# A two-layer RWKV-7 and gMLP trunk: new places and banks in the loop, low-rank products by split halves, gate values projected with tokens on partitions

## The chip, the cores and the metric

The kernel runs on one core of a Trainium2 chip. The metric is the device time of one execution in microseconds, the median over several runs. The engines are TensorE (PE in the profile; its weight loads are PEld), VectorE (DVE), ScalarE (ACT), GpSimd (POOL) and SyncE (SP), which here issues the DMAs (queue SPq).

## The reference

The kernel computes one inference step of two layers with model width D = 1024 and mixer width E = 2048. A prompt of 512 tokens and 8 sample sequences of 4 tokens (32 rows) share the weights. Layer 0 is RWKV-7 time mixing with 32 heads of 64, layer 1 a chunked gMLP.

```python
# layer 0 (h = RMSNorm(x)); sh: first 6272 of 8320 columns, z: the last 2048
proj = h @ w_in
xm = sh + (prev - sh) * mu                   # prev: the token before
r, k, v, wd, ad = split(xm)                  # 2048, 2048, 2048, 64, 64
wf = w0 + tanh(wd) @ w2                      # low-rank products
a  = sigmoid(a0 + ad @ a2)
decay = exp(-exp(-softplus(-wf) - 0.5))
S_t = S_{t-1} diag(w_t) + (S_{t-1} (-kk_t)) (kk_t*a_t)^T + v_t k_t^T
y_t = S_t r_t                                # per head, then group norm, bonus
x  = x + ((norm(y) + bonus) * silu(z)) @ w_out

# layer 1 (h = RMSNorm(x)), chunks of 128 tokens, 8 groups of 256 features
u, v, z = gelu(h @ w_u), gelu(h @ w_v), h @ w_z
v = layernorm(v) * v_g + v_b                 # over the 2048 features of a token
mixed = tril(ws[g]) @ v[chunk, g] + bs       # along the tokens of a chunk
x = x + (u * mixed * silu(z)) @ w_out
```

The outputs are the two final RMSNorms (prompt and sample), the last shifted row and the final matrix state of every sequence, and the sample rows of v.

## The kernel before

**Layout.** The 544 tokens lie on the free axis in two halves of 272 columns (256 prompt, 16 sample); features lie on the 128 partitions. A projection takes a block of 128 features: the weights are the stationary operand and the tokens move. Every fp32 weight and activation is split into a high half (`w_h`, `hh`) and the remainder (`w_l`, `hl`), both of the type fp32r, and a product is made of three matmuls, high x high, high x low, low x high (`mm3`, L249 to L252). `halves` (L115) makes the two halves of a block of weights: a copy on ACT and a subtraction on DVE. A projection of 128 features is 2 halves x 8 blocks of depth x 3 = 48 such matmuls of 272 columns.

**The head** (up to some 40 us) loads x and all constants, norms the tokens, turns them (`pth`) and writes `hh` and `hl`.

**The loop** (some 40 to 730 us) runs over 16 pairs of heads p. Each pair has four projections (k, r, v, z: 192 matmuls), and a list of smaller stages written as generators, which yield after each operation. The names of their PSUM tiles are those of the profile: `plw` and `pla` are the low-rank products (`lora`, L418; 64 rows deep, in fp32, two at once in the upper and lower half of the array), `pge`/`pgo` the Gram products inside a chunk, `pm1` to `pm4` and `pak` the inversion by blocks, `pz`, `pm`, `pn` and `sb` (L795 on) what carries the state from chunk to chunk, `py` the outputs, `psm`, `psy`, `pst`, `psu` the sample rows and their state, `pss` the norms, `pxt` turns of x for later. `pz`, `pm`, `pn`, `py` and the others of a pair of heads use tiles of 64 rows or 64 columns of the array (in the profile 64*128, 128*64 and so on ahead of the shape); `pgs`, `pms` and `pvs` further on use 32.

**What sets the order.** A table `AT` gives for every stage the places of its steps, in units of which a pair of heads has 64 (one unit for 3 matmuls of the projections). All steps are sorted by place into one agenda, and the program is emitted in that order on PE, DVE, ACT, POOL and SP; each engine and queue then works in order. `BANKS` says which of the PSUM banks a stage's tile lies in. After the loop, the output projection (`po`, `out_stream`) is woven in with the last stages: the junction, 720 to 780 us.

**The second layer** first projects the gate values (gv, 16 blocks of 128 features). A block's evacuation (`vevac`, L1223) multiplies by the norm factor `bc` on DVE and applies Gelu on ACT, and one block later `vturn` turns it: four transposes of 128x128 (`pvt`, L1235) into `Vt` with tokens on partitions, and one of the 32 sample rows (`pvs`, L1238) into `Vs`. Then statistics, and blocks of gu and gz (272 columns each) with the mixing between: `mix` (L1301) multiplies `Vt` by the 128x128 mixing matrix `wst` (`pmx`) and the sample rows `Vs` by a 32x32 one, `wsx` (`pms`). Last comes the output projection (go, and `pgl` at the end with 256 moving columns; `pgs` for its sample rows, in four tiles of 128x32 of the array) and the final norm.

Of the kernel before, what the change touches and what calls it, by code (L numbers as in the profile page):

```python
# [14 lines left out]
D = 1024  # L15
# [14 lines left out]
BANKS = {'plw0': 'wa', 'plw1': 'g', 'pla0': 'sm', 'pla1': 's', 'pss': 'g', 'pge0': 'g', 'pge1': 'wa', 'pgo0': 's', 'pgo1': 'wa', 'pbo0': 's', 'pbo1': 'g', 'pbk0': 'g', 'pbk1': 's', 'pv': 'y', 'pat': 'wa', 'pak': 'sm', 'pxt': 'sm', 'psu': 'wa', 'pm1': 'y', 'pm2': 'wa', 'pm3': 'sm', 'pm4': 'sm', 'ps0': 'wa', 'pit': 'wa', 'psy': 'sm', 'pst': 's', 'pso': 'wa', 'psm': 'y'}  # L30
# [36 lines left out]
def build(tc, A, O, off):  # L67
# [5 lines left out]
    with ctx:  # L73
# [62 lines left out]
        with tc.tile_pool(name="st", bufs=1) as st:  # L136
# [13 lines left out]
            Q.dma_start(cst, A["consts"])  # L150
# [4 lines left out]
            raws_in[1] = load_in(1)  # L155
            r1 = st.tile([113, 128], F32, name="r1")
# [45 lines left out]
            mss = [stats(0), stats(1)]  # L202
            V.tensor_scalar(xsh, xs, mss[0][0:32, 2:3], None, op0=ALU.mult)
            scale(0)
            wts0 = halves(*raws_in.pop(0))
            for h in range(2):
                for k in range(KD):
# [10 lines left out]
                    if h == 0 and k == 4:  # L218
                        scale(1)

# [137 lines left out]
        def pcol(col, p):  # L358
            return col[:, p : p + 1]
# [49 lines left out]
        lx = lH.tile([128, 2, HT], F32, name="lx")  # L409
        xl = hd("xl", "h1")  # L410

        def lora_in():
            for js, src in ((slice(0, 256), xl[:, 0:512].rearrange("p (h j) -> p h j", h=2)), (slice(256, 272), xl[:, 512:544].rearrange("p (h j) -> p h j", h=2))):
                S.activation(lx[e_, :, js], src[e_], AF.Tanh)
                S.activation(lx[o_, :, js], src[o_], AF.Copy)
            yield

        def lora(p):  # L418

            z = Z[p]  # L420
            lr = lH.tile([128, 128], F32, name=f"lr{p}", tag="lr", bufs=2)
            for n, rs in (("rw_w2", e_), ("rw_a2", o_)):
                Q.dma_start(lr[rs], A[n][0, :, 128 * p : 128 * p + 128])
            yield
            for h in range(2):
                ps = [bk(f"pl{n}{h}", p)[:, 0:HT] for n in "wa"]
                for x, rs in zip(ps, rw_):
                    T.matmul(x, lr[rs], lx[rs, h, :], start=True, stop=True)
                yield
                if h == 0:  # L430
                    xa = z["xa"] = hd(f"xa{p}", "h1")
                for x, dp_, ds_, bcol in ((ps[0], pv(xw), sv(xw), pcol(w0h, p)), (ps[1], cpv(xa), csv(xa), pcol(w0h, 16 + p))):
                    S.activation(dp_[:, 4 * h : 4 * h + 4, :], x[:, 0:256].rearrange("p (c j) -> p c j", j=64), AF.Tanh, bias=bcol, scale=0.5)
                    S.activation(ds_[:, 4 * h : 4 * h + 4, :], x[:, 256:272].rearrange("p (c j) -> p c j", j=4), AF.Tanh, bias=bcol, scale=0.5)
                    yield
# [536 lines left out]
        def tail(p):  # L972
# [59 lines left out]
            wk=(-24.6703, -13.9502, -10.5009),  # L1032
            wr=(-1.92923, 4.85448, 5.61825),
            wv=(0.606097, 15.3323, 15.3323),
            wz=(26.5557, 37.8471, 43.6636),
            sk=(0.789221, 8.8031, 15.711, 15.8424, 17.6719, 17.7726, 18.4403),
            sr=(7.54549, 28.6206, 31.674, 31.674, 34.0009, 34.0009, 38.5955),
            sv=(43.7782, 45.1654, 47.4232, 49.7307, 49.7307, 51.0746, 55.203),
            sl=(-48.6951, -2.31874, 1.08412, 4.68622, 4.68622, 4.68622, 4.68622),
            lin=(5.21945,),  # L1040
            kpost=(24.9494, 25.986, 25.986, 25.986, 26.4478, 26.4478, 26.4478, 28.1479, 28.7234, 28.9758, 46.1589),
            norms=(26.5963, 27.2646, 42.3595, 42.3595, 43.7228, 43.7228),
            norms0=(30.3638, 36.1029, 36.1029, 42.7321, 43.0652, 43.81),
            rpost=(34.2118, 40.034, 43.0665, 59.6417),
            gram=(38.5207, 38.5207, 38.5207, 38.5207, 38.5507, 38.7256, 44.4019, 46.8335, 55.0017),
            vpost=(57.36,),
            bonus=(47.1621, 50.0087, 67.1245, 68.9711, 69.0871, 71.7472),
            gate=(58.7304, 58.7304, 68.9911, 70.1851, 70.432, 104.018),
            keys=(51.7578, 52.1495, 90.6263, 93.0718),
            sides=(71.9966, 73.0768, 73.0768, 79.7128, 89.332),  # L1050
            lora=(-37.6497, -16.243, -12.6778, -6.32377, -6.32377, -5.15096, 0.12609, 0.958916, 8.84795, 19.5291, 19.5291, 39.8259),
            lora0=(-48.6977, 9.64576, 9.64576, 9.68669, 9.68669, 9.68669, 9.68669, 9.68669, 9.69389, 18.8347, 22.6537, 30.7022),
            lanes=(4.59191, 56.0959, 56.1972, 56.1972, 57.7957, 57.8272, 57.8272, 59.1798, 61.4444, 61.4444, 61.7838, 61.7838, 63.4843, 63.4843, 64.0257, 64.7786, 65.5865, 65.5865, 68.1234, 68.1534, 76.599, 78.8691),
            merge=(89.9516, 90.29, 91.6755, 91.6755, 93.2448, 94.0464, 94.0464, 99.0064, 99.0064, 102.136, 102.373),
            smp=(4.36649, 64.2531, 73.5271, 79.3115, 79.3115, 82.6169, 82.6169, 82.6169, 84.1463, 84.509, 88.3156, 89.5629, 89.5629, 90.1406, 90.873, 93.3779, 94.0364, 99.466, 102.52, 102.958, 103.396, 105.645, 115.209, 116.915, 116.947, 124.943, 129.788, 136.306, 191.625),
            chain=(102.988, 102.988, 102.988, 102.988, 103.098, 104.998, 104.998, 105.819, 111.041, 111.599, 111.599, 111.599, 111.85, 111.85, 111.85, 114.008, 114.008, 114.008, 114.008, 115.066, 115.066, 115.284, 116.962, 118.608, 120.078, 121.408, 121.557, 123.546, 124.856, 128.208, 128.208, 129.056, 129.056, 129.056, 129.847, 129.965, 129.965, 147.17),
            tail=(132.502, 132.502, 132.572, 132.98, 132.98, 141.147, 141.337, 146.854, 147.433, 159.083, 159.098, 163.745, 164.046, 166.048, 166.166, 166.34, 168.968, 171.692),
            flip=(115.408, 135.41, 142.071, 165.144),
# [116 lines left out]
        with tc.tile_pool(name="l1", bufs=1) as l1, tc.tile_pool(name="l1t", bufs=2) as lt, tc.tile_pool(name="ob1", bufs=4) as ob:  # L1175
# [19 lines left out]
            bl = [(0, 0, 128), (0, 128, 128), (1, 0, 128), (1, 128, 128), (0, 256, 16), (1, 256, 16)]  # L1195
            for i, (h, a, n) in enumerate(bl):
                T.matmul(ps[0:n, i : i + 1], acc[:, h, a : a + n], ones[:, 0:1], start=True, stop=True)
            rs1 = l1.tile([128, 6], F32, name="rs1")
            V.tensor_scalar(rs1[:, 0:4], ps[:, 0:4], 1.0 / D, NORM_EPS, op0=ALU.mult, op1=ALU.add)
            V.tensor_scalar(rs1[0:16, 4:6], ps[0:16, 4:6], 1.0 / D, NORM_EPS, op0=ALU.mult, op1=ALU.add)  # L1200
            G.tensor_tensor(out=rs1[:, 0:4], in0=rs1[:, 0:4], in1=nhalf[:, 0:4], op=ALU.pow)
            G.tensor_tensor(out=rs1[0:16, 4:6], in0=rs1[0:16, 4:6], in1=nhalf[0:16, 0:2], op=ALU.pow)
            bc = l1.tile([128, 2, HT], F32, name="bc")
            for h in range(2):
                ps = wa("pbc")
                for i, (hh_, a, n) in enumerate(bl):
                    if hh_ == h:
                        dg = lt.tile([128, 128], F32, name=f"dg{i}", tag="dg")
                        V.tensor_scalar(dg[0:n, 0:n], ident[0:n, 0:n], rs1[0:n, i : i + 1], None, op0=ALU.mult)
                        T.matmul(ps[:, a : a + n], ones[0:n, :], dg[0:n, 0:n], start=True, stop=True)  # L1210
                S.activation(bc[:, h, :], ps[:, 0:HT], AF.Copy)
# [3 lines left out]
            Vs = l1.tile([32, E], F32, name="Vs")  # L1215
# [3 lines left out]
            for f in range(NF):  # L1219
                vT = lt.tile([128, 2, 256], F32, name=f"vT{f}", tag="gz", bufs=3)  # L1220
                vTs = lt.tile([128, 2, 16], F32, name=f"vTs{f}", tag="vTs")

                def vevac(h, ps, f=f, vT=vT, vTs=vTs):  # L1223
                    a = lt.tile([128, HT], F32, name=f"va{f}", tag="va")
                    V.tensor_tensor(out=a, in0=ps, in1=bc[:, h, :], op=ALU.mult)
                    S.activation(vT[:, h, :], a[:, 0:256], AF.Gelu_apprx_tanh)
                    S.activation(vTs[:, h, :], a[:, 256:272], AF.Gelu_apprx_tanh)

                project(f"gv{f}", G_IN, E + 128 * f, vevac)

                def vturn(f=f, vT=vT, vTs=vTs):
                    ps = wa("pvt")
# [13 lines left out]
                if f:  # L1246
                    late()
# [257 lines left out]
```

## Time and profile before

| | before |
|---|---|
| median of 3 runs | 1301.79 us (1300.9 to 1302.03) |
| the profiled execution: its own time, its span | 1303.13 us, 1301.3 us |
| mean granted TensorE clock | 0.996 |
| PE busy | 1272.5 us (98%), 14860 matmuls |
| DVE, ACT, POOL busy | 961.2 (74%), 690.9 (53%), 126.6 (10%) |
| DMA | 123.24 MB, 95 GB/s in the mean |
| PE waiting longest | png on a DMA at the start 8.2; po on DVE's o_l 2.4; pth on xsh 1.7 |

The times below are those of the profiled execution. A line of the timeline or of the groups has the source line, engine, operation, the tile written and the tiles read, for a matmul the part of the array (rows * columns) where it is given, and the shape. The busy time of a matmul includes its way through the array, so successive matmuls overlap, and the distance from start to start says what one costs.

### The profile page before, as it was taken

The numbers are of one execution on the slowest core, as the hardware profiler recorded it, in microseconds if no ns is written. First come the engines' busy times: TensorE is split into PE (matmuls) and PEld (weight loads), VectorE is DVE, ScalarE is ACT, GpSimd is POOL, SyncE is SP. The second block draws the span as 40 slices with busy tenths as digits, with TensorE's granted clock in tenths as the row PEclk, the third lists the DMA queues.
The fourth block names the chain that finished last, engine by engine and source line by source line (L and its number), as shares of the span: only waits on it lengthen the run. The fifth ranks groups of instructions, "written<-read, shape, count | busy, mean of one in ns | idle before, by whom it ended". The sixth has DMA issues, their size and how long they took to land.

```text
span 1301.3 us, 35878 instructions
## 1 busy us (share of the span) xinstructions
PE 1272.5 (98%) x14860; PEld 1200.1 (92%) x14860; DVE 961.2 (74%) x2231; ACT 690.9 (53%) x1612; POOL 126.6 (10%) x346
## 2 busy tenths in 40 slices
PE   6999999999999999999999989999999999999997
PEld 5899999999998999899999879999999999999997
DVE  5688888888888888888888866474448656656466
ACT  5766667667666766766677453254333223232333
POOL 1122011111211110111112100000000000000000
PEclk9999999999999999999999999999999999999999
DMA  4522342433343243424233454332222232232411
GB/s 151 126 74 72 90 118 68 119 79 99 86 110 99 78 109 87 107 64 114 70 83 78 132 162 133 110 96 82 82 82 86 62 107 77 75 101 60 156 37 69
DMA packets 278182, 123.24 MB, mean 95 GB/s; under 512 B 115090, under 2 KB 270884, under 8 KB 278020
## 3 DMA queue, kind: packets, MB, share of 16 engines
q1 hardware_dynamic: 258372, 105.88, 30.0%
q10 hardware_dynamic: 19648, 15.08, 3.9%
q8 instruction: 117, 1.92, 0.6%
q14 instruction: 45, 0.37, 0.1%
HBM read 100.97 MB, written 19.95 MB: 93 GB/s over the span
## 4 chain that ended last, share of the span: by engine, by line
PE 90%; ACT 5%; DVE 2%; DMA 1%; issue 1%; POOL 0%; SPq 0%; ACTq 0%; POOLq 0%; DVEq 0%
PE z_p L250 3%; PE gz_p L250 3%; PE k_p L250 2%; PE gz_p L252 2%; PE k_p L252 2%; PE k_p L251 2%; PE gz_p L251 2%; PE gu_p L250 2%; PE gu_p L252 2%; PE gu_p L251 2%; PE gv_p L251 2%; PE gv_p L252 2%; PE gv_p L250 2%; PE r_p L250 2%; PE z_p L252 2%; PE z_p L251 2%
## 5 line engine op out<-in xcount | busy, mean ns | idle before, releaser
L250 PE MATMUL z_p<-hh,z_h 128*128 128x272 f32 x256 | 81.0, 316 | 0.0
L250 PE MATMUL r_p<-hh,r_h 128*128 128x272 f32 x256 | 77.8, 304 | 0.0
L250 PE MATMUL k_p<-hh,k_h 128*128 128x272 f32 x256 | 77.7, 303 | 0.0
L250 PE MATMUL v_p<-hh,v_h 128*128 128x272 f32 x256 | 76.7, 299 | 0.0
L250 PE MATMUL gv_p<-hh,gv_h 128*128 128x272 f32 x256 | 75.5, 295 | 0.0
L250 PE MATMUL gz_p<-hh,gz_h 128*128 128x272 f32 x256 | 75.5, 295 | 0.0
L251 PE MATMUL gv_p<-hl,gv_h 128*128 128x272 f32 x256 | 74.2, 290 | 0.0
L250 PE MATMUL gu_p<-hh,gu_h 128*128 128x272 f32 x256 | 74.2, 290 | 0.0
L252 PE MATMUL gv_p<-hh,gv_l 128*128 128x272 f32 x256 | 74.1, 289 | 0.0
L251 PE MATMUL gu_p<-hl,gu_h 128*128 128x272 f32 x256 | 73.9, 289 | 0.0
L252 PE MATMUL gu_p<-hh,gu_l 128*128 128x272 f32 x256 | 73.9, 289 | 0.0
L252 PE MATMUL gz_p<-hh,gz_l 128*128 128x272 f32 x256 | 73.9, 289 | 0.0
L252 PE MATMUL z_p<-hh,z_l 128*128 128x272 f32 x256 | 73.9, 289 | 0.0
L252 PE MATMUL k_p<-hh,k_l 128*128 128x272 f32 x256 | 73.8, 288 | 0.0
L252 PE MATMUL r_p<-hh,r_l 128*128 128x272 f32 x256 | 73.7, 288 | 0.0
L252 PE MATMUL v_p<-hh,v_l 128*128 128x272 f32 x256 | 73.7, 288 | 0.0
L251 PE MATMUL gz_p<-hl,gz_h 128*128 128x272 f32 x256 | 73.7, 288 | 0.0
L251 PE MATMUL k_p<-hl,k_h 128*128 128x272 f32 x256 | 73.7, 288 | 0.0
L251 PE MATMUL v_p<-hl,v_h 128*128 128x272 f32 x256 | 73.6, 288 | 0.0
L251 PE MATMUL z_p<-hl,z_h 128*128 128x272 f32 x256 | 73.6, 288 | 0.0
L251 PE MATMUL r_p<-hl,r_h 128*128 128x272 f32 x256 | 73.5, 287 | 0.0
L395 POOL COPY shl<-raw 128x9 f32<-128x9 f32 x49 | 25.5, 520 | 344.7 <-ACT raw L393 344.5
(427 smaller groups left out, 4675.4 us busy)
## 6 DMA issues: line engine op xcount, KB each, us to landing
k_r<-rw_in SPq DMA_DIRECT2D x16, 512.0 KB
r_r<-rw_in SPq DMA_DIRECT2D x16, 512.0 KB
v_r<-rw_in SPq DMA_DIRECT2D x16, 512.0 KB
z_r<-rw_in SPq DMA_DIRECT2D x16, 512.0 KB
gv_r<-gm_in SPq DMA_DIRECT2D x16, 512.0 KB
gu_r<-gm_in SPq DMA_DIRECT2D x16, 512.0 KB
gz_r<-gm_in SPq DMA_DIRECT2D x16, 512.0 KB
go_r<-gm_out SPq DMA_DIRECT2D x24, 256.0 KB
```

Source lines behind the costliest of these rows:

```text
L250: T.matmul(ps, whi, ahi, start=first, stop=False)
L251: T.matmul(ps, whi, alo, start=False, stop=False)
L252: T.matmul(ps, wlo, ahi, start=False, stop=last)
L395: G.tensor_copy(shl[:, :, f], raw[:, 512:553:5])
```

## The change

It has four parts.

1. *The loop's places and banks.* `AT` and `BANKS` have new numbers. (The steps are the same except those of `lora`, which has sixteen where it had twelve.)
2. *The low-rank products.* The 64-row activations are split into high and low halves and stacked on 128 partitions (`lw` for the decay, `la` for a). The weights are loaded on both halves of the partitions, and split; `lrl` holds the remainder against the high half of the activations and zeros against the low half. Two fp32r matmuls on the whole array then make one product of 272 columns.
3. *The second layer's values.* `vproject` takes blocks of 256 features: 128 tokens are stationary (`hh`, `hl`), the weights move in 256 columns, and the result has tokens on partitions, so that the turns go, and Gelu takes the norm factor as its scale (`rs1`). The sample rows come from `hs`, in fp32: 32 columns of the array for each of four pieces of 64 features, 8 blocks of depth, 32 matmuls to a block (`gvs`). The remainders and high halves of the lower 512 rows of weights have one buffer each.
4. *Sample rows on the whole array.* `Vs` and `wsx` are padded with zeros to 128 rows; the norm factor of the sample rows is made for 128 partitions at once; the last turns of the sample rows go from eight to two, those of the shifted rows from nine to four.

In the head, the load of the constants is in two parts, the statistics of the second half of the tokens come after the first half's scaling, its scaling two steps earlier, and the weight halves of the low-rank projection later.

```diff
-BANKS = {'plw0': 'wa', 'plw1': 'g', 'pla0': 'sm', 'pla1': 's', 'pss': 'g', 'pge0': 'g', ...
+BANKS = {'plw0': 's', 'plw1': 'wa', 'pla0': 'g', 'pla1': 's', 'pss': 'sm', 'pge0': 'y', ...
...
-            mss = [stats(0), stats(1)]
+            mss = [stats(0)]
             V.tensor_scalar(xsh, xs, mss[0][0:32, 2:3], None, op0=ALU.mult)
             scale(0)
-            wts0 = halves(*raws_in.pop(0))
+            mss.append(stats(1))
...
-                    if h == 0 and k == 4:
+                    if h == 0 and k == 2:
                         scale(1)
+                    if h == 0 and k == 6:
+                        wts0 = halves(*raws_in.pop(0))
...
         def lora_in():
+            for js, src in parts:
+                S.activation(xlc[e_, :, js], src[e_], AF.Tanh)
+            S.activation(lw[e_], xlc[e_], AF.Copy)
+            V.tensor_tensor(out=ll[e_], in0=xlc[e_], in1=lw[e_], op=ALU.subtract)
+            for js, src in parts:
+                S.activation(la[o_, :, js], src[o_], AF.Copy)
+                V.tensor_tensor(out=ll[o_, :, js], in0=src[o_], in1=la[o_, :, js], op=ALU.subtract)
+            for rs, os, x in ((e_, o_, lw), (o_, e_, la)):
+                S.activation(x[os], ll[rs], AF.Copy)
...
+            lrh = lH.tile([128, 2, 128], F32R, name=f"lrh{p}", tag="lrh", bufs=2)
+            S.activation(lrh, lr, AF.Copy)
+            yield
+            lrl = lrls[p % 2]
+            for i, rs in enumerate((e_, o_)):
+                V.tensor_tensor(out=lrl[rs, i, :], in0=lr[rs, i, :], in1=lrh[rs, i, :], op=ALU.subtract)
+            yield
...
+            def down(h, i, x, ps):
+                ps[h] = bk(f"pl{'wa'[i]}{h}", p)[:, 0:HT]
+                T.matmul(ps[h], lrh[:, i, :], x[:, h, :], start=True, stop=False)
+                T.matmul(ps[h], lrl[:, i, :], x[:, h, :], start=False, stop=True)
...
-                ps = [bk(f"pl{n}{h}", p)[:, 0:HT] for n in "wa"]
-                for x, rs in zip(ps, rw_):
-                    T.matmul(x, lr[rs], lx[rs, h, :], start=True, stop=True)
...
-            lora=(-37.6497, -16.243, -12.6778, -6.32377, -6.32377, -5.15096, 0.12609, ...
+            lora=(-54.2734, -17.5215, -15.1165, 2.26593, 2.48318, 2.73372, 2.73372, ...
...
-                project(f"gv{f}", G_IN, E + 128 * f, vevac)
...
-                        T.transpose(ps[:, 128 * j : 128 * j + 128], vT[:, j // 2, 128 * (j % 2) : 128 * (j % 2) + 128], ident)
...
+            def vproject(q):
...
+                        hi = vw.tile([128, 4, 256], F32R, name=f"gv{q}_h", tag="whB")
+                        lo = vw.tile([128, 4, 256], F32R, name=f"gv{q}_l", tag="wlB")
...
+                for k in range(KD):
+                    hi, lo = (x[:, k % 4, :] for x in w[k // 4])
+                    for i in range(4):
+                        o = ps[i // 2][:, 256 * (i % 2) : 256 * (i % 2) + 256]
+                        ah, al = tile_(hh, k, i), tile_(hl, k, i)
+
+                        T.matmul(o, ah, hi, start=k == 0 and i % 2 == 0, stop=False, skip_group_check=True)
+                        T.matmul(o, al, hi, start=False, stop=False, skip_group_check=True)
+                        T.matmul(o, ah, lo, start=False, stop=k == KD - 1, skip_group_check=True)
+                pss = p1.tile([128, 512], F32, tag="sm", name="gvs")
+                for k in range(KD):
+                    for j in range(4):
+                        T.matmul(pss[32 * j : 32 * j + 32, 0:64], hs[:, k, :], raws_[k // 4][:, k % 4, 64 * j : 64 * j + 64], start=k == 0, stop=k == KD - 1, skip_group_check=True)
+                for i in range(4):
+                    S.activation(Vt[:, i, 256 * q : 256 * q + 256], ps[i // 2][:, 256 * (i % 2) : 256 * (i % 2) + 256], AF.Gelu_apprx_tanh, scale=rs1[:, i : i + 1])
+                for j in range(4):
+                    c = 256 * q + 64 * j
+                    S.activation(Vs[0:32, c : c + 64], pss[32 * j : 32 * j + 32, 0:64], AF.Gelu_apprx_tanh, scale=rs1[32 * j : 32 * j + 32, 4:5])
```

**PE in the loop before, where the fifth pair's low-rank products stand.** `pn` (of an earlier pair) closes the matmuls that prepare the carrying of the state; the first pair of low-rank products stands behind it, then z's projection, and between two steps of the carrying (`sb`) the two state updates of the sample rows. Numbers behind a name tell tiles of one name apart.

```order
L823 MATMUL pm_2949<-GK_2018,XA_2871 64x128
L829 MATMUL pn_2964<-W_2453,GK_2018 64x64 x16
L428 MATMUL plw_2982<-lx,lr_2633 128x272
L428 MATMUL pla_2983<-lx,lr_2633 128x272
L250 MATMUL z_p<-hh,z_h 128x272
L251 MATMUL z_p<-hl,z_h 128x272
L252 MATMUL z_p<-hh,z_l 128x272
...
L854 MATMUL sb_3014<-RS_2947,MB 128x64
L952 MATMUL pst_3018<-We_2881,BT_2512 128x256
L952 MATMUL psu_3019<-We_2881,BT_2512 128x256
L854 MATMUL sb_3022<-RS_2947,MB 128x64
```

The matmuls of the same names after, two pairs later (the loop repeats itself):

```order
L255 MATMUL v_p<-hh,v_l 128x272
L988 MATMUL pst_4607<-We_4481,BT_4060 128x256
L988 MATMUL psu_4608<-We_4481,BT_4060 128x256
L859 MATMUL pm_4618<-GK_3697,XA_4564 64x128 x2
...
L865 MATMUL pn_4633<-W_4201,GK_3697 64x64 x16
L253 MATMUL v_p<-hh,v_h 128x272
```

The state updates `pst` and `psu` now stand ahead of `pm` with no projection between, and `pn` is followed by a projection. The seventh pair's low-rank products come later, among the matmuls of k, on the whole array:

```order
L255 MATMUL k_p<-hh,k_l 128x272
L456 MATMUL plw_4809<-lw,lrh_4611 128x272
L457 MATMUL plw_4809<-lw,lrl_322 128x272
L456 MATMUL pla_4814<-la,lrh_4611 128x272
L457 MATMUL pla_4814<-la,lrl_322 128x272
L253 MATMUL k_p<-hh,k_h 128x272
```

Here no instruction between two of the projection uses a part of the array.

**PE in the second layer's values, before**, with a block's turn in the middle of the next block's projection:

```order
L252 MATMUL gv_p<-hh,gv_l 128x272
L1235 MATMUL pvt<-cst,vT_14433 128x128 x4
L1238 MATMUL pvs<-cst,vTs_14434 32x128
L1269 MATMUL psh<-cst,shl 49x128 x4
L250 MATMUL gv_p<-hh,gv_h 128x272
```

After:

```order
L1294 MATMUL gv_p<-gv_h,hh 128x256
L1295 MATMUL gv_p<-gv_h,hl 128x256
L1296 MATMUL gv_p<-gv_l,hh 128x256
L1300 MATMUL gvs<-gv_0_r,hs 32x64 x16
L1300 MATMUL gvs<-gvb_r,hs 32x64 x16
L1318 MATMUL prs<-wst,ones 128x512 x2
```

The turns are gone, the 32 matmuls of the sample rows stand at the end of each block of 256 features, and operands of the projection have changed sides.

More of the change, by code (lines that the diff above doesn't have):

```diff
@@ L1040, in build @@
[L1040 to L1047, printed above, removed]
@@ L1194, in build @@
             ps = wa("pn1")
[L1195 to L1200, printed above, removed]
@@ L1201, in build @@
-            G.tensor_tensor(out=rs1[:, 0:4], in0=rs1[:, 0:4], in1=nhalf[:, 0:4], op=ALU.pow)
-            G.tensor_tensor(out=rs1[0:16, 4:6], in0=rs1[0:16, 4:6], in1=nhalf[0:16, 0:2], op=ALU.pow)
+            accs = l1.tile([128, 4, 2, 16], F32, name="accs")
+            G.tensor_copy(accs, acc[:, None, :, 256:272].to_broadcast([128, 4, 2, 16]))
+            for i in range(4):
+                T.matmul(ps[:, i : i + 1], acc[:, i // 2, 128 * (i % 2) : 128 * (i % 2) + 128], ones[:, 0:1], start=True, stop=True)
@@ L1203, in build @@
+            T.matmul(ps[:, 4:5], accs.rearrange("p a h j -> p (a h j)"), ones[:, 0:1], start=True, stop=True)
+            rs1 = l1.tile([128, 5], F32, name="rs1")
+            V.tensor_scalar(rs1, ps[:, 0:5], 1.0 / D, NORM_EPS, op0=ALU.mult, op1=ALU.add)
+            G.tensor_tensor(out=rs1, in0=rs1, in1=nhalf[:, 0:5], op=ALU.pow)
             bc = l1.tile([128, 2, HT], F32, name="bc")
+            dgs = l1.tile([128, 32], F32, name="dgs")
+            V.tensor_scalar(dgs, ident[:, 0:32], rs1[:, 4:5], None, op0=ALU.mult)
@@ L1204, in build @@
             for h in range(2):
                 ps = wa("pbc")
[L1206 to L1210, printed above, removed]
+                for i in range(2):
+                    dg = lt.tile([128, 128], F32, name=f"dg{h}{i}", tag="dg")
+                    V.tensor_scalar(dg, ident, rs1[:, 2 * h + i : 2 * h + i + 1], None, op0=ALU.mult)
+                    T.matmul(ps[:, 128 * i : 128 * i + 128], ones, dg, start=True, stop=True)
@@ L1211, in build @@
+                T.matmul(ps[:, 256:272], ones, dgs[:, 16 * h : 16 * h + 16], start=True, stop=True)
                 S.activation(bc[:, h, :], ps[:, 0:HT], AF.Copy)
             Vt = l1.tile([128, 4, E], F32, name="Vt")
-            Vs = l1.tile([32, E], F32, name="Vs")
+            Vs = l1.tile([128, E], F32, name="Vs")
+            G.memset(Vs, 0.0)
+            wsx = l1.tile([128, 8, 8, 4], F32, name="wsx")
+            G.memset(wsx, 0.0)
             bst = l1.tile([128, 5, 4, 6], F32, name="bst")
@@ L1249, in build @@
+            for f in range(8):
+                vproject(f)
                 if f == 0:
```

186 lines of the change are left out of this document (106 added, 80 removed).

## The prediction, made before the changed kernel ran

> **What bounds the kernel now.** I read the page first: the share of busy time, then the chain that ended last.
>
> ```profile
> PE 1272.5 (98%) x14860; PEld 1200.1 (92%) x14860; DVE 961.2 (74%) x2231; ACT 690.9 (53%) x1612; POOL 126.6 (10%) x346
> PE 90%; ACT 5%; DVE 2%; DMA 1%; issue 1%; POOL 0%; SPq 0%; ACTq 0%; POOLq 0%; DVEq 0%
> ```
>
> TensorE is both the busiest engine and nine tenths of the chain. The windows say where it is not; the columns are the stretch in us, busy time of PE, PEld, DVE, ACT and POOL, the granted clock, DMA share and GB/s.
>
> ```profile
> 300.00:400.00 100.00, 99.78 (x1549) 91.92 (x1548) 86.78 (x217) 69.00 (x175) 15.77 (x47) 1.00 0.35 92
> 720.00:740.00 20.00, 17.34 (x219) 15.23 (x217) 17.85 (x49) 9.18 (x24) 2.58 (x4) 1.00 0.49 144
> 740.00:760.00 20.00, 16.86 (x168) 15.49 (x169) 14.50 (x35) 9.89 (x21) 1.80 (x1) 0.86 0.72 191
> 760.00:780.00 20.00, 18.02 (x315) 16.24 (x313) 12.88 (x32) 11.16 (x30) 0.00 (x0) 0.97 0.46 141
> ```
>
> Inside the loop PE is full (99.78 of 100) and DVE is next (86.78). Only the junction between the loop and the second layer has holes: 60 less 17.34, 16.86 and 18.02 leaves 7.8 us, and the clock dips to 0.86 there. So the question is what the change does to PE's own work. Busy time cannot answer it, because a matmul of 0.29 us is shown while the next one starts 0.126 us later. I take start-to-start steps from the timeline. Its columns are start, duration, engine, line, operation and tiles.
>
> ```profile
> 60.11 0.28 PE L252 MATMUL z_p<-hh,z_l 128*128 128x272 f32 x1
> 60.32 0.49 PE L428 MATMUL plw<-lx,lr 64*128 64x272 f32 x1
> 60.66 0.39 PE L428 MATMUL plw<-lx,lr 64*128 64x272 f32 x1
> 60.98 0.39 PE L250 MATMUL z_p<-hh,z_h 128*128 128x272 f32 x1
> 61.21 0.29 PE L251 MATMUL z_p<-hl,z_h 128*128 128x272 f32 x1
> 63.23 0.29 PE L252 MATMUL z_p<-hh,z_l 128*128 128x272 f32 x1
> ```
>
> From 61.21 to 63.23 stand 16 steps: 0.126 us for a split product of 272 columns. The low-rank pair (plw and pla side by side, two passes each) takes 60.32 to 60.98, 0.66 us. But from the last z_p ahead of it to the second z_p behind it are 1.10 us where two steps would be 0.25, so the pair costs 0.85. The missing 0.19 is paid for going into a smaller array tile and out again. I call it a stretch of small tiles, at 0.2 us.
>
> **Part by part: the low-rank products.** Each of 16 head pairs has two such pairs: 32 x 0.66 = 21.1 us. They become 8 split products of 272 columns on the whole array, 128 x 0.126 = 16.1. **-5.0 us.** The new halves cost ACT one copy and DVE two subtractions per head pair, beside PE.
>
> **The loop's places.** The period is 45.03 us by two rows of the chain:
>
> ```profile
> 267.78 1.10 PE pz L803 x32
> 312.81 1.10 PE pz L803 x32
> ```
>
> By the order, PE enters small tiles ten times per head pair before (pz; pm, pn and a low-rank pair; pst and psu; the second pair; py; psm; pm with pak and pss; pm; pm; pm with the Gram products) and six times now: the low-rank pairs are gone as tiles, pst and psu stand directly ahead of pm and pn, psm directly ahead of py, and pz directly behind the Gram products, where psy stood between. Four stretches x 16 x 0.2 = **-12.8 us**; with the 5.0, 1.1 us a period. If only the two stretches of the low-rank pairs pay, it is -6.4; the order shows all four gone, so I keep 12.8. What hides the new waits is DVE's slack: 86.78 of 100 is 39.1 us in 45.03; with two subtractions more (I put 0.4 us for both) it is 39.5 in 43.9. I add **+2** for waits that a fuller DVE will show in 16 periods; the bounds are 0 and the whole 17.8 (a rival below).
>
> **Second layer's values.** A block of 128 features ends in a turn today:
>
> ```profile
> 894.74 0.29 PE L252 MATMUL gv_p<-hh,gv_l 128*128 128x272 f32 x1
> 894.87 0.60 PE L1235 MATMUL pvt<-cst,vT 128*128 128x128 f32 x4
> 895.30 0.27 PE L1238 MATMUL pvs<-cst,vTs 128*32 128x128 f32 x1
> 895.54 0.29 PE L251 MATMUL gv_p<-hl,gv_h 128*128 128x272 f32 x1
> 901.32 0.29 PE L252 MATMUL gv_p<-hh,gv_l 128*128 128x272 f32 x1
> ```
>
> 894.74 to 895.54 is 0.80; less two steps, the turn costs 0.55. Sixteen go: **-8.8 us.** The 768 split products keep their number but move 256 columns instead of 272. The old step is (901.32 - 895.54) / 46 = 0.1257. The new one stands in the last projection of this same kernel:
>
> ```profile
> 1277.82 0.28 PE L1409 MATMUL pgl<-gl_hi,goh 128*128 128x256 f32 x1
> 1280.88 0.28 PE L1411 MATMUL pgl<-gl_hi,gol 128*128 128x256 f32 x1
> 1281.09 1.93 PE L1450 MATMUL pgs<-xT,gos 128*32 128x256 f32 x32
> 1282.95 0.38 PE L1409 MATMUL pgl<-hh,goh 128*128 128x256 f32 x1
> 1283.17 0.28 PE L1410 MATMUL pgl<-hl,goh 128*128 128x256 f32 x1
> ```
>
> Its 26 steps take 3.06, 0.1177 each: 768 x 0.008 = **-6.1 us.** The sample rows are added: per block of 256 features, 8 rounds of four 128x32 tiles with 64 moving columns and two passes. pgs is the same form with 4 rounds of 256 columns: 1280.88 to 1283.17 less two steps is 2.05, less 0.2 for the stretch 0.46 a round, so 0.115 for 64 columns if time goes with columns. The nearest row with 64 columns is dearer:
>
> ```profile
> 138.52 1.08 PE pn L829 x32
> 872.41 0.86 PE prs L1253 x2
> ```
>
> pn runs 8 rounds of two 128x64 tiles, 0.135 each. So a block costs 8 x 0.115 to 8 x 0.135 plus 0.2, 1.1 to 1.3; I take 1.2, times 8: **+9.6 us.** That the tiles overlap at all is in prs: a pass of 512 columns takes 0.43, so 256 take 0.215, and pgs's 32 passes in 1.86 are 8 x 0.23, four side by side.
> The upper bound is no overlap, by a pair of passes of 65 columns on the whole array:
>
> ```profile
> 70.98 0.33 PE L905 MATMUL psm<-cst,VU 128*128 128x65 f32 x2
> 71.15 0.28 PE L906 MATMUL psm<-cst,BD 128*128 128x128 f32 x1
> ```
>
> 0.085 a pass, 64 passes and the stretch: 5.6 a block, +45.
> A rule of the Trainium skill speaks for that bound: "TensorE: Matmul & The Clock Gate", in the section on packing small matmuls, says that a weight load overlaps running matmuls only when the row groups differ, and these four tiles share all rows. By it every load of the eight in a round would stand bare and the sum would be the slower rival's below; pgs's 0.23 a round speaks against it at 256 columns, and no row shows it at 64.
>
> The weight halves of a block's second half have one buffer: ACT's and DVE's conversion waits for the block's last matmul, then for four Gelu reads. What covers it is the sample block and the next block's first 48 products, 1.2 + 5.6 us; the turn of one 128x1024 half is about 2.3 us behind some 2.5 of reads. I cost it at nothing; uncovered it would be at most 3 us in seven blocks.
>
> **Sample rows by the whole array.** In the mixing, the sample product used a 32-row tile behind eight passes of 128 columns:
>
> ```profile
> 993.16 0.29 PE L252 MATMUL gu_p<-hh,gu_l 128*128 128x272 f32 x1
> 993.29 1.05 PE L1307 MATMUL pmx<-wst,Vt 128*128 128x128 f32 x8
> 994.27 0.40 PE L1308 MATMUL pms<-wsx,Vs 32*128 32x32 f32 x2
> 994.60 0.39 PE L250 MATMUL gz_p<-hh,gz_h 128*128 128x272 f32 x1
> 994.84 0.29 PE L251 MATMUL gz_p<-hl,gz_h 128*128 128x272 f32 x1
> ```
>
> 993.16 to 994.84 less two steps is 1.43. On the whole array the eight passes stay 0.9 (0.98 without the way into the tile), and two short ones are 0.17 by the 65-column pair: 1.07. Sixteen times 0.36: **-5.8 us.** The smaller edits (six final transposes fewer, five in the shift output, two broadcasts without 16-row tiles) go together at some ten transposes of 0.11 and four stretches of 0.2: **-2 us**, bounds -3 and 0.
>
> **The head.** Two effects of opposite sign:
>
> ```profile
> 16.53 1.22 DVE L119 TENSOR_TENSOR lora_l<-lora_r,lora_h 128x1024 fp32r<-128x1024 f32 x1
> 17.67 0.16 DVE L194 TENSOR_SCALAR ms<-ms 128x2 f32<-128x2 f32 x1
> 18.72 1.15 ACT L199 ACTIVATE xh<-xt,ms 128x1024 f32<-128x1024 f32 x1 [0.90 <-POOL ms L195]
> 33.74 0.62 ACT L414 ACTIVATE lx<-xl 64x512 f32<-64x512 f32 x1
> 49.53 0.46 PE L548 MATMUL pgo<-AR,BK 64*128 64x128 f32 x2 [1.12 <-DVE AR L520]
> ```
>
> The second half's scale (18.72) stood behind lora_l on DVE (16.53 to 17.67); now its statistics come first: about -2. But the first head pair's chain is late already (PE waits 1.12 at 49.53), and its input now takes three more copies of 0.62 on ACT before the first low-rank product: +2. Queued behind that product on PE are k, r and v. I take **0**, bounds -3 and +5. The junction's holes (7.8 us and the slower clock) are ordered by the same rules as before; **0**, bounds -6 and +6.
>
> **The sum:** -5.0 - 12.8 + 2 - 8.8 - 6.1 + 9.6 - 5.8 - 2 = -28.9. The profiled span is 1301.3 (its run 1303.13), so 1272.4; the median of the runs is 1301.79, half a microsecond over the span: **1273 us**.
>
> **The rivals.** *The loop gains nothing, 1291 us.* DVE idles 5.9 us in a period of 45.03. If that idle time is not slack but the sum of its waits in line with PE, the period stays and only the second layer gains: 1273 + 17.8. For it: in-order queues on four engines, rearranged. Against: PE has hardly a hole in 100 us.
> *Slower, 1308 us.* The sample rows' four tiles do not overlap at 64 columns, 5.6 us a block instead of 1.2: 1273 + 8 x 4.4. It decides once a block costs over 4.8 us. Against it stand pn and pgs.
> *The junction closes, 1263 us.* With fewer stretches the last head pairs finish sooner, its 7.8 us and the slow clock go: 10 us less. Against: those waits name DVE and DMA, which the change leaves.
>
> **How the numbers follow.** The forecast 0.61, with its own range of 1265 to 1282 from the bounds of head and junction; the idle loop 0.17; the closed junction 0.08; the slower one 0.08; a mixture that ends between forecast and no change 0.06. The range from 1261 to 1292 takes in the forecast and both neighbours. Faster by over 0.2% (about what a measurement here can tell from none) is 0.89 (all but the slower case and half of the mixture), within 0.2% 0.03 (that half), slower 0.08.
>
> **What would show it.** In the changed profile: a period of 43.9 us between two pz with PE still over 99% busy; steps of 0.118 in gv_p and a sample block of 1.1 to 1.3 us; no transposes of vT; 1.1 us from pmx to the next projection. It is wrong if PE shows holes of 0.5 us and more in every period with DVE named, if a sample block is over 2 us, or if the junction's idle grows by more than 6.

## The result, and the profile after

The changed kernel takes 1279.16 us (median of 4 runs, 1277.68 to 1281.38) against 1301.91 before: ratio 0.9828, 95% interval 0.9811 to 0.9845. The prediction was 1273, its range 1261 to 1292. The profiled execution's span went from 1301.3 to 1275.8. That is 25.5 us, where the medians differ by 22.8: the profiled execution of before lay 1.2 us above its median, that of after 1.5 below (1277.68).

The page of the changed kernel, the busy time and the chain:

```profile
PE 1244.5 (98%) x15279; PEld 1194.8 (94%) x15279; DVE 955.3 (75%) x2210; ACT 692.6 (54%) x1613; POOL 134.9 (11%) x346
PE 87%; issue 5%; DVE 3%; ACT 2%; DMA 1%; POOL 0%; ACTq 0%; SPq 0%; POOLq 0%; DVEq 0%
```

PE has 419 matmuls more and is busy 28 us less, at the same share. The 5% "issue" is time in which the chain waited for nothing that the profile shows. The chain, by the rows of `pz`, gives the periods of the loop:

```profile
262.73 1.03 PE pz L839 x32
306.79 1.03 PE pz L839 x32
...
483.09 1.03 PE pz L839 x32
531.56 1.03 PE pz L839 x32
575.22 1.03 PE pz L839 x32
```

A period is 44.06 us (45.03 before), and 43.65 past the tenth (44.61 before). But the tenth, 483.09 to 531.56, takes 48.47. The windows (start and end, then busy time of PE, PEld, DVE, ACT, POOL, the granted clock, DMA share, GB/s):

```profile
300.00:400.00 100.00, 100.00 (x1532) 94.30 (x1533) 90.57 (x225) 70.23 (x182) 15.93 (x45) 1.00 0.37 95
500.00:520.00 20.00, 17.80 (x184) 16.82 (x183) 14.33 (x33) 14.12 (x34) 0.33 (x2) 0.91 0.52 122
720.00:740.00 20.00, 15.00 (x156) 13.70 (x155) 16.59 (x44) 7.94 (x18) 0.00 (x0) 0.91 0.67 193
```

DVE fills 90.57 of 100, up from 86.78, and PE has no hole there. There is a new one at 500 to 520, and the clock falls to 0.91 behind it. The junction's holes are still there, 7.7 us from 720 to 780 (7.8 before), now 5.0 of them in the first third.

Between the same marks of the two profiled executions (starts of the named matmuls), the difference splits like this:

| stretch | before | after | difference |
|---|---|---|---|
| start to the first pz | 88.0 | 86.8 | -1.2 |
| 13 periods (all but the tenth and the last) | 583.4 | 570.9 | -12.5 |
| the tenth period | 45.4 | 48.5 | +3.1 |
| the last period, with the junction's start | 53.2 | 49.7 | -3.4 |
| last pz to the first gv_p | 92.6 | 92.7 | +0.1 |
| first gv_p to the first gu_p (values) | 112.1 | 107.5 | -4.6 |
| first gu_p to the last matmul | 320.0 | 313.0 | -7.0 |

### The profile page after: what moved, and what is told of

It reads as the page before. It is cut to its first block, busy times and chain, and to the rows that moved or that the text cites. A ratio compares the mean times of both kernels' runs of the same rounds, so it can differ in the third digit from the quotient of the medians.

```text
span 1275.8 us, 36576 instructions
## 1 busy us (share of the span) xinstructions
PE 1244.5 (98%) x15279; PEld 1194.8 (94%) x15279; DVE 955.3 (75%) x2210; ACT 692.6 (54%) x1613; POOL 134.9 (11%) x346
## 4 chain that ended last, share of the span: by engine, by line
PE 87%; issue 5%; DVE 3%; ACT 2%; DMA 1%; POOL 0%; ACTq 0%; SPq 0%; POOLq 0%; DVEq 0%
PE r_p L253 3%; PE v_p L253 3%; PE gz_p L253 3%; PE gz_p L255 3%; PE gu_p L253 3%; PE z_p L253 3%; PE gz_p L254 3%; PE gu_p L255 3%; PE gu_p L254 3%; PE r_p L255 2%; PE r_p L254 2%; PE k_p L253 2%; PE v_p L254 2%; PE v_p L255 2%; PE gv_p L1294 2%
## 5 line engine op out<-in xcount | busy, mean ns | idle before, releaser
L253 PE MATMUL z_p<-hh,z_h 128*128 128x272 f32 x256 | 77.7, 303 | 0.0
L1294 PE MATMUL gv_p<-gv_h,hh 128*128 128x256 f32 x256 | 73.4, 287 | 0.0
L1296 PE MATMUL gv_p<-gv_l,hh 128*128 128x256 f32 x256 | 72.1, 282 | 0.0
L1295 PE MATMUL gv_p<-gv_h,hl 128*128 128x256 f32 x256 | 71.9, 281 | 0.0
L255 PE MATMUL go__p<-goh,go_l 128*128 128x272 f32 x192 | 55.6, 289 | 0.0
```

The lines of the kernel that those rows point to most:

```text
L253: T.matmul(ps, whi, ahi, start=first, stop=False)
L255: T.matmul(ps, wlo, ahi, start=False, stop=last)
L1294: T.matmul(o, ah, hi, start=k == 0 and i % 2 == 0, stop=False, skip_group_check=True)
L1295: T.matmul(o, al, hi, start=False, stop=False, skip_group_check=True)
L1296: T.matmul(o, ah, lo, start=False, stop=k == KD - 1, skip_group_check=True)
```

## The experiments

Periods below are read as above, from rows of `pz` in the loop's middle; a block's price is the distance from the last projection matmul ahead of it to the second behind it, less two steps.

### The low-rank products, undone at the new places

```diff
-                T.matmul(ps[h], lrh[:, i, :], x[:, h, :], start=True, stop=False)
-                T.matmul(ps[h], lrl[:, i, :], x[:, h, :], start=False, stop=True)
...
+                for x, rs in zip(ps, rw_):
+                    T.matmul(x, lr[rs], lx[rs, h, :], start=True, stop=True)
```

> The changed kernel with the low-rank products of before (fp32, two side by side on 64 rows each) at the new places. Theory: a pair of passes takes 0.66 us where four split products take 0.50, and each pair is a stretch of small tiles of its own (two more in a period): 2 x 0.16 + 2 x 0.2 = 0.7 us a period, 44.76, time 1279 + 11 = 1290. Rival: stretches cost nothing by themselves: 0.3 us a period, 44.38, time 1284.

1286.56 us, ratio 0.9882 (0.9859 to 0.9905). The chain:

```profile
313.04 1.03 PE pz L810 x32
357.88 1.03 PE pz L810 x32
```

44.84 us, 0.78 more than the changed kernel; 0.7 was expected, so stretches cost what the first theory said. A pair on PE, in the timeline:

```profile
373.88 0.29 PE L255 MATMUL k_p<-hh,k_l 128*128 128x272 f32 x1
374.10 0.49 PE L433 MATMUL plw<-lx,lr 64*128 64x272 f32 x1
...
375.06 0.29 PE L254 MATMUL k_p<-hl,k_h 128*128 128x272 f32 x1
```

373.88 to 375.06 less two steps of 0.125 is 0.93; the second pair of the period costs 0.86. The total moved by 7.4 (the profiled spans by 10.7) and not by 11; a part of it is the tenth period, 46.4 here and not 48.5.

### The places and banks, undone

```diff
-            lora=(-54.2734, -17.5215, -15.1165, 2.26593, ...
+            lora=(-37.6497, -24.0, -20.0, -16.243, ...
```

(and all other rows of `AT`, and `BANKS`, as before the change; places and banks were undone together, so what each of the two does alone stays open)

> The changed kernel with the banks and places of before (those of the new steps of the low-rank products put where the old ones stood). Theory: small tiles cost per stretch, 0.2 us; this kernel has nine stretches in a period where the changed one has six and the kernel before ten: period 44.06 + 0.6 = 44.66, and the wait of the tenth period goes, since the turns of x stand elsewhere: 1279 + 9.6 - 4.2 = 1285. Rival: the new places gain by closing waits between engines: then PE shows waits of 0.3 us and more in every period here, with DVE or ACT named. Second rival: the low-rank products make all of the gain: period 44.1, time 1275.

1299.07 us, ratio 0.9972 (0.9954 to 0.9990): nearly all of the gain is gone, more than any of the theories said. The chain's period is 45.37, longer than before the change, and the waits name why:

```profile
PE pm L859 <- ACT W L848: 8.4, 15, 0.6
```

15 waits of 0.56 us for a copy on ACT. In this run the new copy of the low-rank weights stood right beside it, which was the choice of the experiment. The next run has their load, copy and subtraction some 20 units earlier:

```diff
-            lora=(-37.6497, -24.0, -20.0, -16.243, ...
+            lora=(-56.0, -45.0, -43.0, -16.243, ...
```

> As the run with the places of before, but the copy and the subtraction of the low-rank weights stand 20 units earlier on ACT and DVE. In that run the period was 45.4 us and PE waited 0.56 us in each for W, the copy of which stood beside the new copy of the low-rank weights on ACT. Theory: that wait came from where the new steps were put: without it the period is 44.85 (44.06 and three stretches at 0.26), time 1290. Rival: the old places leave ACT too late for W whatever is put beside: period 45.3 and more, 1298.

1292.87 us, ratio 0.9923 (0.9900 to 0.9947); the wait for `W` is gone.

```profile
317.65 1.10 PE pz L839 x32
362.59 1.10 PE pz L839 x32
```

The period is 44.94, 0.09 above what was expected, and the first theory holds for that wait. (The total is 3 us over the forecast, and this run loses 5 us ahead of the first pz, 93.4 for 88.0, probably by the same move.) The four kernels make a square:

| period, us | places of before | new places |
|---|---|---|
| low-rank products of before | 45.03 | 44.84 |
| split low-rank products | 44.94 | 44.06 |

Each part alone gains 0.1 to 0.2, both together 0.97. So the two together gain some 0.7 more than apart, and most of that can be read from the rows. The old pairs are cheap at the old places, where one of them follows `pn`, another stretch of small tiles, and the other stands between two `sb`. There the first costs 0.66 us (`pm`, `pn` and the pair 3.14; with two split products in its place, in the last run, 2.73, less their 0.25) and the second 0.80. At the new places, where each stands alone among k's matmuls, they cost 0.93 and 0.86: 0.33 more.

Another part is a wait that the last run still has, in every period, and that neither the kernel before nor the changed one has:

```profile
326.22 0.28 PE L255 MATMUL z_p<-hh,z_l 128*128 128x272 f32 x1
326.62 0.41 PE L890 MATMUL sb<-RS,MB 128*128 128x64 f32 x2
```

`sb` starts 0.40 us behind the projection where a step is 0.125, so 0.27 us are idle. It reads `RS`, which DVE finishes only at 326.48; that this is the cause is read from the rows and not tested. Without it the period would be 44.67, and the split products alone would gain 0.36 at the old places. The two parts do gain more together, but by 0.4 rather than 0.7.

The new places also close a wait, which the kernel before has in every period and the runs with its places keep:

```profile
317.12 0.38 ACT L812 ACTIVATE W<-pz 64x256 f32<-64x256 f32 x1
317.15 0.29 PE L252 MATMUL v_p<-hh,v_l 128*128 128x272 f32 x1
317.55 1.09 PE L823 MATMUL pm<-GK,XA 64*64 64x128 f32 x28
```

`pm` starts 0.40 us behind the projection, where the way into a small tile takes 0.21 at other places, and right behind the last copy of `W` on ACT (317.50). With `pst` and `psu` ahead of `pm` these 0.19 us are filled. The rival of the run with the old places, that the new ones close waits between engines, is therefore right for 0.19 of the 0.97; below the 0.3 that it named.

### The values, undone

```diff
-            for f in range(8):
-                vproject(f)
...
+                project(f"gv{f}", G_IN, E + 128 * f, vevac)
```

> The changed kernel with the gate values projected as before (features on partitions, 272 columns, a turn for each of 16 blocks). Theory by the prediction's terms: 8.8 + 6.1 - 9.6 = 5.3 us more, 1284.5; by the steps of the two traces 768 x 0.0072 + 8.8 - 9.8 = 4.5, 1283.7. Rival: the new projection's gain was already lost to its buffers or evacuations: 1279.

1281.51 us, ratio 0.9838 (0.9823 to 0.9852). In the trace, first gv_p to first gu_p is 111.0 us where the changed kernel has 107.5: 3.5 dearer, of the 4.5 that the steps give. So the gain is there, and its buffers or evacuations took at most 1 us of it; the medians, 2.4 apart with 4 runs each, say no more.

### The sample rows' four pieces in one part of the array

```diff
-T.matmul(pss[32 * j : 32 * j + 32, 0:64], hs[:, k, :], ...
+T.matmul(pss[0:32, 64 * j : 64 * j + 64], hs[:, k, :], ...
```

> The changed kernel; the four pieces of 64 features of the sample rows' product all use the first 32 columns of the array, instead of 32 columns each. Theory: the four overlap in the changed kernel (1.22 us a block) and cannot here: 64 passes at 0.085 and the stretch are 5.6 us a block, time 1279 + 35 = 1314. Rival: the passes go at their own rate whatever their columns are: 1.2 us a block, 1279.

1301.49 us, ratio 0.9994 (0.9981 to 1.0007). A block in the changed kernel and here, by the timeline:

```profile
904.39 0.28 PE L1296 MATMUL gv_p<-gv_l,hh 128*128 128x256 f32 x1
904.59 0.65 PE L1300 MATMUL gvs<-gv_r,hs 128*32 128x64 f32 x32
905.06 0.63 PE L1300 MATMUL gvs<-gvb_r,hs 128*32 128x64 f32 x32
905.62 0.39 PE L1294 MATMUL gv_p<-gv_h,hh 128*128 128x256 f32 x1
905.85 0.28 PE L1295 MATMUL gv_p<-gv_h,hl 128*128 128x256 f32 x1
```

```profile
914.92 0.28 PE L1296 MATMUL gv_p<-gv_l,hh 128*128 128x256 f32 x1
915.12 1.97 PE L1300 MATMUL gvs<-gv_r,hs 128*32 128x64 f32 x32
916.94 1.95 PE L1300 MATMUL gvs<-gvb_r,hs 128*32 128x64 f32 x32
918.82 0.39 PE L1294 MATMUL gv_p<-gv_h,hh 128*128 128x256 f32 x1
919.04 0.28 PE L1295 MATMUL gv_p<-gv_h,hl 128*128 128x256 f32 x1
```

904.39 to 905.85 less two steps of 0.12 is 1.22 us; with one part of the array the same 64 passes take 3.88 us (914.92 to 919.04 less two steps). So the four do overlap, which saves 8 x 2.66 = 21.3 us; the spans differ by 23.5. The size expected, 5.6 a block, was too high: a pass alone costs 0.058 (915.12 to 918.82, by 64), not 0.085.

### The mixing's sample rows on 32 rows again

```diff
-T.matmul(ps2[:, 0:32], Vs[:, fs_], wsx[:, g] ...
+T.matmul(ps2[:, 0:32], Vs[0:32, fs_], wsx[0:32, g] ...
```

> The changed kernel with the sample rows of the mixing on 32 rows of the array again (the same two passes). Theory: 16 stretches come back: by the prediction 16 x 0.36 = 5.8 us, by the two traces (1.675 and 1.368 us from the last projection ahead to the second behind) 16 x 0.31 = 4.9: time 1284. Rival: the stretch costs only where PE is short of work behind it: 1280 at most.

1284.19 us, ratio 0.9857 (0.9841 to 0.9873); first gu_p to the end is 317.5 us against 313.0. The block is 1.675 again at all 16 places: 4.6 us in the stretch, 5.0 in the medians. The first theory holds, with the traces' 4.9 and not the prediction's 5.8.

### The hole in the tenth period

Here is the new hole, in the changed kernel's timeline (start, duration, engine, where ACTq and SPq are the queues on which ACT and SP issue DMAs; in brackets the idle time ahead and what ended it):

```profile
502.80 1.86 SPq L824 DMA_DIRECT2D xfd<-xo  x1
...
505.78 3.31 SPq L725 DMA_DIRECT2D dz<-lz  x1
...
511.06 0.34 ACTq L1159 DMA_DIRECT2D ofl<-od  x1
511.46 0.47 ACT L460 ACTIVATE xa<-pla,w0h 128x256 f32<-128x256 f32 x1 [3.35 <-issue]
511.54 1.28 SPq L729 DMA_DIRECT2D Zf<-dz  x2
...
512.15 0.39 PE L618 MATMUL pbo<-rkh,bo 128*128 128x272 f32 x1 [2.20 <-ACT xa L461]
```

PE waits 2.20 us for `xa`. ACT stands idle for 3.35 us, from 508.1 on: it issues a load of `ofl` first, and that load needs a buffer whose last content, the turned sample rows of x, is stored by L824; by the order of the rows it waits for that store. Before the change the same load also came behind that store (522.70 and 527.73), at a place where PE waited for nothing of ACT's. These loads are work for the output projection, 200 us later. Four runs followed the wait.

*The small rows of the store.*

```diff
-on(p, "flip", flip(p - 1))
+on(p, "flip", flip(KD if p == 1 else p - 2))
```

> The changed kernel, but of the nine turns of x in the loop the one of the sample rows goes first and not last. Theory: in the changed kernel the tenth period (483.02 to 531.49, 48.47 us where its neighbours take 44.1 and 43.7) holds a wait of 2.20 us (pbo at 512.15), because the ACT queue's second load of ofl waits for a buffer whose store, 2048 pieces of 64 bytes issued at 502.80, is still on its way, and the tanh of xa stands behind that load; a stretch of half clock (3.41 us) follows it. With the turns of the prompt last, that store is one of long rows: the wait and the half clock go, the period is 43.7 to 44.2, the time 4 us less, 1275. Rival: the traffic of that moment (v_r, lr, sn) delays the load whichever store stands ahead of it: the wait stays over 1.5 us, the time 1279.

1281.25 us, ratio 0.9843 (0.9817 to 0.9868): no gain.

```profile
514.39 0.39 PE L618 MATMUL pbo<-rkh,bo 128*128 128x272 f32 x1 [2.09 <-ACT xa L461]
```

The wait is the same with a store of long rows: that theory fell, and any store at this place seems to hold the load. (No half clock followed here, and the tenth period is 46.6. The second and the fifth are 1.0 and 1.3 us longer than their neighbours; in both `pm` waits for DVE's `T`, 0.61 and 1.22 us, as it does in the runs below. The second is where the store of the sample rows now stands, and the issue of dz's store behind it takes 2.92 us there.)

*The loads on SP.*

```diff
-            OQ.dma_start(src, od[k])
+            (Q if k < 2 else OQ).dma_start(src, od[k])
```

> The changed kernel; only the first two loads of ofl are issued by SP and not by ACT (they then stand between the store of dz and the load of Zf). With the sample rows' turn put first, the load still waited until 512.78 behind a store issued at 505.41, and pbo waited 2.09 us: so it is not the small rows of the store, but that any load on ACT at this place waits for a store to land, with the tanh of xw and xa behind it. Theory: with the loads on SP, pbo waits no more, the tenth period is 44.1 us, no half clock near 512, and the time is 2 to 4 us less: 1276. Rival: the load of Zf, now behind them on SP, is late instead, and pz or psy waits 1 us and more: 1279.

1278.60 us, ratio 0.9815 (0.9800 to 0.9829). `pbo` waits 0.2 us at most, but the rival is half right:

```profile
PE pm L750 <- DVE T L740: 1.6, 1, 1.6
```

`Zf`, behind the loads on SP, is loaded 2.1 us later (513.65), and `pm` waits for what is made of it. The tenth period is 46.1.

*The loads two pairs later*, by steps of their own in the agenda (792 is place 24 of the twelfth pair, 12 x 64 + 24):

```diff
...
+        for k, u in ((0, 792), (1, 792)):
+            agenda.append((u, len(agenda), (0, "fetch", k), fetch(k)))
```

> The changed kernel; the first two loads of ofl are issued by SP two pairs of heads later (at place 12 x 64 + 24, behind the load of Zf), when the store whose buffer they take has long landed. With the loads on SP right behind the store, pbo waited no more, but the load of Zf came 2.1 us later (513.65 for 511.54) and pm waited 1.6 us for T. Theory: now neither waits; the period that follows 483 is 44.1 us; against the changed kernel 4.4 us less in that period, of which 1.7 are a half clock that does not come in every execution: time 1275 to 1277. Rival: some other wait at that place, as the stores of the sample state, holds the tenth period over 45.5 us: 1278 and more.

1275.25 us, ratio 0.9789 (0.9769 to 0.9809). The tenth period is 45.63, just over the rival's 45.5, though the time is the theory's. One wait is left:

```profile
517.66 0.27 PE L750 MATMUL pm<-T,GK 64*64 64x64 f32 x1 [1.15 <-DVE T L740]
```

*And the store behind the load of Zf*, as it stood before the change (on top of the run with the two loads later):

```diff
-            for n, u in enumerate(AT[stage]):
+            for n, u in enumerate(AT[stage][:3] + (150.0,) if (stage, p) == ("flip", 9) else AT[stage]):
```

> As the run with the two loads two pairs later, and the store of the sample rows of x (2048 pieces of 64 bytes) stands behind the load of Zf on SP and not ahead of the store of dz (before the change it stood behind both). In that run pbo waited no more, but pm waited 1.15 us at 517.66 for T, and the issue of dz's store took 3.04 us where it takes 0.9 in other pairs. Theory: the store ahead of it held dz up: now no wait is left at that place, the tenth period is 44.1 to 44.3, time 1.4 us less than that run, 1274. Rival: dz and Zf are late for the load of v and the states, which stay ahead of them: period 45 and more, 1275.

1275.83 us, ratio 0.9817 (0.9803 to 0.9831). SP's queue, and the chain's tenth period:

```profile
507.30 0.63 SPq L725 DMA_DIRECT2D dz<-lz  x1
510.38 1.28 SPq L729 DMA_DIRECT2D Zf<-dz  x2
511.75 0.58 SPq L824 DMA_DIRECT2D xfd<-xo  x1
```

```profile
484.62 1.03 PE pz L839 x32
529.03 1.03 PE pz L839 x32
```

44.41 us, 0.1 over the theory's bound, and PE has no wait in it. The store of dz is issued in 0.63 us where it took 3.31. So the hole is settled by its periods: 48.47, 45.63 without the loads on ACT, 44.41 with the store out of the way too. In time, the medians of these last two kernels are 3.9 and 3.3 us under the changed kernel's. But each ratio is to the kernel before as timed beside that run, and by the ratios (0.9789 and 0.9817 against 0.9828) only the interval of the first lies wholly under the changed kernel's. The second's overlaps it: its shorter period is seen in the trace, and not in the time.

### The junction

*The subtraction of two blocks on POOL* (on top of the sample rows' turn first):

```diff
+split(ah[:, i], al[:, i], h2(src), G if k in (2, 3) else V)
```

> As the run with the sample rows' turn first, and at the junction the remainders of the third and fourth block of the output projection (ol) are subtracted on POOL and not on DVE. Theory: po waits 3.44 us at 727.78 in the changed kernel because ol stands behind the last lanes on DVE (721.95 to 727.0), and a half clock of 3.41 us follows: both go, 3 to 5 us less than the run without it, about 1271. Rival: what is behind (the last pair's lanes, its inverse, the sample rows) sets the end of the junction anyway, or POOL is slow on 128x544: within 1 us of the run without it, 1275.

1281.50 us, ratio 0.9846 (0.9823 to 0.9868), no gain over 1281.25. POOL's rows:

```profile
725.59 3.87 POOL L1149 TENSOR_TENSOR ol<-ofl,oh 128x544 fp32r<-128x544 f32 x2 [5.22 <-ACT oh L1148]
```

1.9 us for each where DVE takes 0.71: waits of 1.45 and 1.52 us stand in place of the one of 3.51 in the run that it was built on.

*The loads of those blocks without waiting for a buffer* (on top of the two loads later):

```diff
+            if k in (2, 3):
+                v = xT[:, 4 + k]
+                OQ.dma_start(v.rearrange("p h j -> p (h j)"), od[k])
+                return split(ah[:, i], al[:, i], v)
```

> As the run with the two loads later, and the third and fourth block of the output projection's input are loaded into a part of xT not yet in use, so that they need not wait for the first two buffers (in the changed kernel they were issued at 720.41, behind the subtractions of the first two). Theory: po's wait of 3.44 us at 727.78 shrinks by 1 to 2 us, since DVE's lanes still stand ahead of two of the subtractions: 1274 to 1276. Rival: DVE's order alone sets it: as the run with the two loads later.

1281.16 us, ratio 0.9833 (0.9813 to 0.9854), dearer than without it.

```profile
726.21 0.59 PE L254 MATMUL po<-ol,o_h 128*128 128x272 f32 x1 [4.32 <-DVE ol L1158]
```

One wait of 4.32 where there were 1.11 and 3.67: the rival's mechanism is right, DVE's order sets it (the subtraction stands behind the last pair's reductions). It named the time of the run without it, and the medians are 5.9 us apart. The two profiled spans differ by 3.9, of which 1.8 lie ahead of the first `pz` and 1.9 in the last period, where `pat` waits 1.54 us for DVE; why is open.

## Why the prediction was right, and where not

**The loop** was to gain 17.8 in 16 periods less 2 for waits, 0.99 a period; it gained 0.97 in all but one. That the two numbers meet is partly luck. The 17.8 are 1.11 a period, and 0.97 came without any wait for DVE, so the terms were 0.14 a period too large, 2.2 in all, and the 2 put in for waits stood in their place. And 0.19 of the 0.97 is the closed wait ahead of `pm`, which is in no term. By the rows the low-rank products went from 1.46 us a period to 1.06, 0.40, where their term and one of the four stretches make 0.51; that leaves 0.38 for the other three stretches, put at 0.6. Nor do the two terms stand by themselves. "-5.0" for the low-rank products and "-12.8" for four stretches were worked out as if each part kept its gain without the other. The square says 0.09 (0.36 without the wait for `sb`) and 0.19 a period for each alone, 0.97 for both.

The rival of the idle loop is out: it had the period stay, and the period shrank with PE full. (Its 1291 adds all of the 17.8 to a forecast that had the 2 for waits in it; with them taken back it is 1289.)

**The stretch** at 0.2 us was right in size for a pair that stands alone among projection matmuls, but not what the prediction took it for, a price of the smaller tile alone. After small tiles the second projection matmul follows the first by 0.23 us instead of 0.125; after fp32 matmuls on the whole array (`pbk`, `sb`, `pit`) by 0.21; after fp32r ones (`pbo`, the new `plw` and `pla`) by 0.13. So most of the way out is paid on returning from fp32 to fp32r, whatever the tile, and only the way in, some 0.08 us, belongs to the tile. Rows of before and of after show it:

```profile
323.10 0.61 PE L610 MATMUL pbk<-cst,BK 128*128 128x128 f32 x4
323.46 0.37 PE L250 MATMUL z_p<-hh,z_h 128*128 128x272 f32 x1
323.67 0.28 PE L251 MATMUL z_p<-hl,z_h 128*128 128x272 f32 x1
```

```profile
367.44 0.28 PE L457 MATMUL pla<-la,lrl 128*128 128x272 f32 x1
367.56 0.29 PE L253 MATMUL k_p<-hh,k_h 128*128 128x272 f32 x1
367.69 0.28 PE L254 MATMUL k_p<-hl,k_h 128*128 128x272 f32 x1
```

That also fits the three stretches at 0.38: those that were joined, or lay beside other fp32 work, saved some 0.13 each. Split halves lose both ways because they are whole-array *and* fp32r. No run changed only the type, so this is read from rows and not tested.

**"+2 for waits that a fuller DVE will show in 16 periods"** is the step that failed. DVE, at 90.57 of 100, caused none in the other periods. The price fell in one place, 4.4 us in the tenth period (48.47 for 44.06), and there a load on ACT's queue was the cause. A part of it is the stretch of half clock, which the same hole did not bring in every run: with the values or the mixing undone the loop is the same and its granted clock is 1.00 from 500 to 520, and the tenth period is 47.2. The prediction looked at what stands on PE and at DVE's busy time, and not at what the new places put ahead of whom on the queues that issue DMAs. With this hole away the profiled span would be 1275.8 - 4.4 = 1271.4, against 1272.4 predicted; the last kernel of that series, which has no wait there, came to 1274.0 in its profiled execution, with a head 1.4 us longer.

**The values:** -5.3 predicted, -4.6 in the trace. The turn was 0.55, the sample block 1.22 (1.1 to 1.3 predicted), the step 0.1185 and not 0.1177: 8.8 + 5.5 - 9.8 = 4.5, so the step is nearly all of what is missing. The run with the values undone showed 3.5 of it; where the microsecond between went is open, and it bounds what the single buffers cost. The rule of the Trainium skill ("TensorE: Matmul & The Clock Gate", packing small matmuls), that weight loads overlap running matmuls only when the row groups differ, does not agree with the trace, as the prediction applied it: four tiles that share all rows and differ in columns take 1.22 us, one tile 3.88. The slower rival had this mechanism but its size was wrong too: without overlap a block is 3.88, under the 4.8 from which it would have decided.

**The mixing:** -5.8 predicted, 16 x 0.307 = -4.9 measured. The term left out the way back from fp32 (the step of 0.21), which the whole array pays too. **The smaller edits** are taken as the rest of the last stretch, 7.0 - 4.9 = 2.1, where -2 was predicted; no run undid them.

**The head** is -1.2 in the profiled pair, but the same head ends between 86.8 and 89.3 us in the runs above, so this is not told from 0. **The junction** kept its waits for DVE, as said against the rival that closes it; the last period gained 2.4 us beside its share.

## What to carry to other kernels

Where one engine is full, count start-to-start steps and the forms of the instructions around them: a product in another type or on a part of the array costs its own time and a change of form on either side, and a rearrangement that groups such forms may only pay together with one that removes them. After a reordering, check each queue that issues DMAs for a transfer that waits for a buffer ahead of urgent work on the same engine; a prefetch for 200 us later cost 2 to 4 us there, and moving it gave that back in the period. Two gains worked out from the same rows are to be tried alone as well as together before they are added.

## What the runs showed of the hardware that was not expected

- On PE the step from the first to the second projection matmul was 0.21 us behind fp32 work on the whole array and 0.13 behind fp32r work, against 0.125 within a projection of 272 columns.
- Behind a store of 2048 pieces of 64 bytes the issue of the next store on the same queue took 3.31 us (3.04 with the loads moved away); with that store moved behind it, 0.63.
- After the hole of 2.20 us PE ran at half clock for 3.41 us (from 512.9) in the changed kernel. The same wait of `pbo` was 2.50 us with a half clock behind it in one other run, and 2.09, 2.37, 2.39 and 2.74 us without one in four, so its length does not decide it.
- POOL took 1.9 us for a subtraction of 128x544 that DVE does in 0.71.
